# Three of eight groups of w_down as seven products in chained PSUM banks, on a hybrid decoder trunk

## The chip, the cores and the metric

The kernel runs on one core of one Trainium2 chip. The metric is the device time of one execution in microseconds (us); the lower, the better.

## The reference

Two layers of a decoder trunk over 576 token columns (512 of a prompt, 64 of eight samples). Each layer mixes the tokens with four kinds of heads and then runs an MLP of 1024 to 4096 to 1024. The change touches the MLP alone:

```python
x = x + jnp.einsum('ble,ed->bld', mix, P['w_out'][li])
h2 = rmsnorm(x, P['norm_mlp_w'][li])
up = jnp.einsum('bld,df->blf', h2, P['w_up'][li])
x = x + jnp.einsum('blf,fd->bld', jnp.square(jax.nn.relu(up)), P['w_down'][li])
```

## The kernel before

**Layout and arithmetic.** Activations lie with features on the 128 partitions and the 576 columns in the free dimension, in two halves of `TH` = 288. `x` is eight tiles of 128 features. Every fp32 operand of a large product is split into a high part (ScalarE casts it to fp32r) and a low part (VectorE subtracts the high part), and one 128x128 block of a product is three matmuls: high by high, high by low, low by high, each over 288 columns.

**The MLP.** There are 32 tiles of hidden features ("middle tiles"). `mlp` makes them two at a time (a pair, 16 pairs a layer); four of them are a group, and `w_down` is applied group by group, eight groups a layer, one group behind the pairs that are being made. The last group of the last layer goes through `last_down`, which also does the final norm.

**w_up.** The first three pairs of a layer are made plainly (`up_tile`). The other 13 go through `up_pair`: a pair is a 2 by 2 arrangement (two middle tiles, two halves of columns), and seven products of 12 matmuls replace eight (Strassen's form as Winograd orders it). The sums of weights are made on VectorE (lines 1085 to 1088), the sums of activations once a layer (`quads`). Each of the seven products has a PSUM bank of its own out of five in rotation (`bank`); VectorE adds the products into the four quarters (`add`, line 1108), multiplies by the norm's factor under a relu (line 1111), and ScalarE squares (line 1147). The halves are split and stored as `fh`, `fl`.

**w_down.** Per group there are four weight blocks (`m2`) of 128x1024. For each, `down` makes four products of 12 matmuls (two output tiles, two halves). Each has a PSUM bank out of three in rotation (`mmbank`), and VectorE adds the bank to `x` (line 1037).

**Order and buffers.** A scheduler sets each engine's order when the program is built; the order is fixed then, and every engine works through its queue in that order. `high_priority` moves the splits and the take-up of banks ahead. A raw weight tile (SyncE's queue loads it) has three buffers (`raw`), a split plain weight two (`hi`, `lo`), the split weights of `up_pair` three (`uh`, `ul`), its last one (`vh`, `vl`) and its sums (`s`) one.

Of the kernel before, what the change touches and what calls it, by code (L numbers as in the profile page):

```python
# [10 lines left out]
F32 = mybir.dt.float32  # L11
# [8 lines left out]
DEPTH = 2  # L20
# [21 lines left out]
PLAIN, QUADS = 3, 1  # L42
SA, SC = 1, 2
# [105 lines left out]
class Kern:  # L149
# [481 lines left out]
    def dt_proj(self):  # L631
# [410 lines left out]
    def quads(self, P):  # L1042
# [3 lines left out]
        for k in range(4):  # L1046
# [5 lines left out]
            t1 = P.t(("U", "W", "T1a", "T1b")[k], TH)  # L1052
# [18 lines left out]
    def up_pair(self, P, i, Q, rstd):  # L1071
# [3 lines left out]
        hl = lambda n, w, b: (P.t(n + "h", [w, 128], F32R, b), P.t(n + "l", [w, 128], F32R, b))  # L1075

        def split(hl, src):
            S.copy(hl[0], src)  # L1078
            V.tensor_tensor(hl[1], src, hl[0].bitcast(F32), op=ALU.subtract)
            return hl  # L1080

        with self.tc.high_priority(HP):
            a = split(hl("u", 8, 3), ra)
            s = P.t("s", [8, 128])
            V.tensor_tensor(s[:, :4], rb[:, :4], rb[:, 4:], op=ALU.add)
            V.tensor_tensor(s[:, 4:], s[:, :4], ra[:, :4], op=ALU.subtract)
            V.tensor_tensor(rb[:, :4], ra[:, :4], rb[:, :4], op=ALU.subtract)
            V.tensor_tensor(ra[:, 4:], ra[:, 4:], s[:, 4:], op=ALU.subtract)
            s = split(hl("u", 8, 3), s)
            b = split(hl("u", 8, 3), rb)  # L1090
            d = split(hl("v", 4, 1), ra[:, 4:])

        out = [[self.fp.t(n, dt=F32R, bufs=8) for n in ("fh", "fl")] for _ in range(2)]
        rs = [rstd[:, :TH], rstd[:, TH:]]

        def mul(n, w, o, q):
            ps = self.bank(n)
            j = 0
            for k in range(4):
                (wh, wl), (xh, xl) = (t[:, o + k] for t in w), Q[q][k]  # L1100
                for u, x in ((wh, xh), (wh, xl), (wl, xh)):
                    nc.tensor.matmul(ps[:, :TH], u, x, start=j == 0, stop=j == 11)  # L1102
                    j += 1
            return ps[:, :TH]

        def add(out, x, y):
            with self.tc.high_priority(HP):
                V.tensor_tensor(out, x, y, op=ALU.add)

        def relu(c, m, h):  # L1110
            V.scalar_tensor_tensor(c, c, 0.0, rs[h], op0=ALU.max, op1=ALU.mult)
            self.square(c, out[m], h)
# [282 lines left out]
```

## Time and profile before

| | us |
|---|---|
| median of three runs (1357.02 to 1363.0) | 1357.02 |
| the profiled execution | 1355.2 |
| its span, first to last instruction | 1353.4 |
| PE (matmul) busy | 1328.0 (98% of the span) |
| PEld (weight load) busy | 1279.6 (95%) |
| DVE (VectorE) busy | 1028.5 (76%) |
| ACT (ScalarE) busy | 658.2 (49%) |

The span is what the trace covers; 1.8 us of the profiled execution lie around it. An engine's busy time is the sum of its instructions' times, overlaps counted once. Matmuls overlap one another, so a busy PE says that it is never without one, and not how fast they follow each other; that is read from the starts in the timeline. "A <- B" in a view of waits says that A's engine stood idle until B was done.

### The profile page before, as it was taken

What the parts mean: (1) busy time and instruction counts of PE and PEld (TensorE: products, weight loads), DVE (VectorE), ACT (ScalarE), POOL (GpSimd) and SP (SyncE); (2) the same over time, 40 slices, a digit from 0 to 9 for tenths busy, and PEclk for the clock granted to TensorE, in tenths of its full rate; (3) what the DMA queues carried; (4) which work ended last, traced back from release to release, by engine and by line L of the source; (5) the groups of instructions that cost most, each with busy time, mean ns of one, the idle gap of its engine ahead of it and who ended that gap; (6) DMA issues with size and microseconds to landing.
All of it is one profiled execution on the core that took longest, in us unless ns stands there. A gap on an engine that the chain in (4) does not pass through costs nothing.

```text
span 1353.4 us, 25452 instructions
## 1 busy us (share of the span) xinstructions
PE 1328.0 (98%) x10384; PEld 1279.6 (95%) x10384; DVE 1028.5 (76%) x2043; ACT 658.2 (49%) x1175; POOL 63.3 (5%) x126
## 2 busy tenths in 40 slices
PE   7999999999999999999999999999999999999997
PEld 7999899799999999999999998988999999999997
DVE  7788888488678677776669678886977677777755
ACT  6565436766243334333354774477653243334325
POOL 2201102000000000000000001100000000000000
PEclk9999999999999999999999999999999999999999
DMA  6324414123213222322331233231223213222312
GB/s 237 104 87 139 165 68 144 48 79 110 77 65 110 78 92 81 113 75 86 131 121 47 98 117 128 94 111 48 79 81 123 78 63 109 79 82 91 115 58 71
DMA packets 39831, 131.36 MB, mean 97 GB/s; under 512 B 6089, under 2 KB 8241, under 8 KB 39681
## 3 DMA queue, kind: packets, MB, share of 16 engines
q1 hardware_dynamic: 29312, 102.12, 21.9%
q0 software_dynamic: 6512, 22.64, 5.0%
q10 hardware_dynamic: 3888, 4.97, 1.2%
q8 instruction: 82, 1.34, 0.4%
q14 instruction: 37, 0.30, 0.1%
HBM read 120.32 MB, written 11.34 MB: 97 GB/s over the span
## 4 chain that ended last, share of the span: by engine, by line
PE 86%; DVE 7%; ACT 3%; issue 2%; DMA 0%; SPq 0%; DVEq 0%; ACTq 0%
PE pd L339 33%; PE p L1102 21%; PE pi L339 15%; PE pu L339 6%; PE pl L1255 2%; PE sc L554 2%; DVE lo L326 1%; DVE a L444 1%; PE ss L402 1%; PE ao L354 1%; ACT hi L326 1%; DVE A L562 1%; DVE qE L550 1%; PE y L354 1%; PE lg L978 1%
## 5 line engine op out<-in xcount | busy, mean ns | idle before, releaser
L326 ACT CAST hi<-raw 128x1024 fp32r<-128x1024 f32 x134 | 140.2, 1046 | 297.1 <-PE pd L339 144.6
L339 PE MATMUL pd<-fh,hi 128*128 128x288 f32 x960 | 284.1, 296 | 0.0
L339 PE MATMUL pd<-fl,hi 128*128 128x288 f32 x960 | 284.0, 296 | 0.0
L339 PE MATMUL pd<-fh,lo 128*128 128x288 f32 x960 | 282.8, 295 | 0.0
L339 PE MATMUL pi<-xh,hi 128*128 128x288 f32 x704 | 210.6, 300 | 7.6 <-ACT xh L377 7.1
L339 PE MATMUL pi<-xl,hi 128*128 128x288 f32 x704 | 210.4, 300 | 1.1 <-DVE xl L378 1.1
L339 PE MATMUL pi<-xh,lo 128*128 128x288 f32 x704 | 211.1, 300 | 0.0
L326 DVE TENSOR_TENSOR lo<-raw,hi 128x1024 fp32r<-128x1024 f32 x134 | 163.6, 1222 | 27.3 <-ACT hi L326 26.7
L1037 DVE TENSOR_TENSOR x<-x,pd 128x288 f32<-128x288 f32 x240 | 108.2, 451 | 97.9 <-PE pd L339 97.8
L339 PEld LDWEIGHTS pd<-fh,lo 128*128 128x128 f32 x960 | 180.9, 188 | 0.0
L339 PEld LDWEIGHTS pd<-fh,hi 128*128 128x128 f32 x960 | 180.4, 188 | 0.0
L339 PEld LDWEIGHTS pd<-fl,hi 128*128 128x128 f32 x960 | 180.4, 188 | 0.0
L339 PEld LDWEIGHTS pi<-xh,hi 128*128 128x128 f32 x704 | 133.0, 189 | 10.1 <-ACT xh L377 7.1
L339 PEld LDWEIGHTS pi<-xh,lo 128*128 128x128 f32 x704 | 132.9, 189 | 6.0 <-issue 5.2
L339 PEld LDWEIGHTS pi<-xl,hi 128*128 128x128 f32 x704 | 132.9, 189 | 3.6 <-DVE xl L378 1.7
L1102 PE MATMUL p<-Th,ul 128*128 128x288 f32 x312 | 92.2, 296 | 0.0
L1102 PE MATMUL p<-Tl,uh 128*128 128x288 f32 x312 | 92.1, 295 | 0.0
L1102 PE MATMUL p<-Th,uh 128*128 128x288 f32 x312 | 92.0, 295 | 0.0
L1102 PE MATMUL p<-xl,uh 128*128 128x288 f32 x312 | 91.9, 295 | 0.0
L1102 PE MATMUL p<-xh,ul 128*128 128x288 f32 x312 | 91.9, 295 | 0.0
L1102 PE MATMUL p<-xh,uh 128*128 128x288 f32 x312 | 91.7, 294 | 0.0
L1078 ACT CAST uh<-raw 128x1024 fp32r<-128x1024 f32 x52 | 54.5, 1048 | 66.8 <-PE p L1102 43.2
(489 smaller groups left out, 3003.2 us busy)
## 6 DMA issues: line engine op xcount, KB each, us to landing
raw<-in_wu SPq DMA_DIRECT2D x64, 512.0 KB, 3.3
raw<-in_wd SPq DMA_DIRECT2D x64, 512.0 KB, 4.2
raw<-in_wi SPq DMA_DIRECT2D x44, 512.0 KB, 3.3
raw<-in_wo SPq DMA_DIRECT2D x16, 512.0 KB, 3.2
x<-in_xT SPq DMA_DIRECT2D x8, 288.0 KB, 5.9
a<-acd ACTq DMA_DIRECT2D x4, 576.0 KB, 4.5
xl<-in_xT POOLq DMA_DIRECT2D x8, 288.0 KB, 4.3
xd<-x POOLq DMA_DIRECT2D x8, 288.0 KB, 2.4
```

The source lines that it names most:

```text
L326: self.split_ins = nc.scalar.copy(hi, raw).ins, nc.vector.tensor_tensor(lo, raw, hi.bitcast(F32), op=ALU.subtract).ins
L339: self.nc.tensor.matmul(out, w, x[:, a], start=n == 0, stop=n == last)
L354: self.nc.tensor.matmul(out, w, x, start=n < 2, stop=n >= len(products) - 2, skip_group_check=True)
L402: nc.tensor.matmul(ps[:, :TH], ones, s[:, TH * h : TH * h + TH], start=n == 0, stop=n == len(sqs) - 1)
L444: V.scalar_tensor_tensor(dst[:, :CW], src[:, k : k + CW], w(k), dst[:, :CW], op0=ALU.mult, op1=ALU.add)
L550: V.tensor_tensor(qE[r, d, : W // 2].rearrange("p (n h) -> p n h", h=h), qu[r], eu[r], op=ALU.mult)
L554: nc.tensor.matmul(pv[:, :, 64 * ci : 64 * ci + 64], kE[:, 128 * ci : 128 * ci + 128], qE[:, :, 64 * ci : 64 * ci + 64], start=True, stop= ...
L562: V.copy_predicated(Av[:, d], m, ps[:, d].rearrange("p (n h) -> p n h", h=h))
L1037: self.nc.vector.tensor_tensor(y[:, a], x[:, a], ps, op=ALU.add)
L1078: S.copy(hl[0], src)
L1102: nc.tensor.matmul(ps[:, :TH], u, x, start=j == 0, stop=j == 11)
L1255: nc.tensor.matmul(ps, u[:, o + q], v[:, a], start=j == 0, stop=j == 11)
```

## The change

**w_down.** In groups 1, 3 and 5 (`SEVEN`) of each layer a weight block is applied by `group_seven`: the two pairs of middle tiles are the two steps of the sum over features, the output is two tiles by two halves, and seven products of six matmuls each replace the eight of that size that `down` makes in four banks. In this text the products of one block are A1, B2, A3, C4, A5, C6, A7, in the order of the code. They share three banks: A1, A3, A5 and A7 accumulate in one bank (`dA`), C4 and C6 in another (`dC`). After each product VectorE adds the bank as it stands to a quarter of `x`, and the next product of the chain goes on accumulating in the same bank. So a block has 42 matmuls and seven adds, where it had 48 and four. The sums of weights are made in place in the raw tile (`sums`, four instructions of 256 columns) and split besides (`vh`, `vl`, 768 columns, one buffer).

**The middle tiles.** A pair is now one tile of up to seven blocks (`Hh`, `Hl`, three buffers of pairs). For the three groups `finish` makes, besides the four squared quarters, three sums of them (four subtractions of 288 columns) and splits all seven. For the other groups the four quarters are split in two instructions of 576 columns. In `mlp` group g is applied after pair 2g + 2 was made (before: after pair 2g + 3).

**w_up.** `up_pair` has three banks in place of seven products' own: four products accumulate in `A`, two in `C`, one is in `B`. After each of A's first three products ScalarE copies the bank as it stands (`U1`, `U`, `W`), and A goes on accumulating. VectorE makes three adds and three relu instructions a pair (before: seven and four).

**Besides.** Two tiles move to another pool (`w4`, `dtq`), the scratch of the software DMA is halved, the output tiles of `last_down` take the buffers of `Th` and `Tl`, and `w_down`'s rows are laid out by pairs.

The diff, cut to its core:

```diff
+SEVEN = (1, 3, 5)
 ...
+    def mul(self, ps, w, o, xs, last=True, first=True):
+        j, n = 0, 3 * len(xs) - 1
+        for k, (xh, xl) in enumerate(xs):
+            wh, wl = (t[:, o + k] for t in w)
+            for u, x in ((wh, xh), (wh, xl), (wl, xh)):
+                self.nc.tensor.matmul(ps, u, x, start=first and j == 0, stop=last and j == n, skip_group_check=True)
+                j += 1
+    def sums(self, s, r, n):
+        V = self.nc.vector
+        q = lambda t, i: t[:, n * i : n * i + n]
+        V.tensor_tensor(q(s, 0), q(r[1], 0), q(r[1], 1), op=ALU.add)
+        V.tensor_tensor(q(s, 1), q(s, 0), q(r[0], 0), op=ALU.subtract)
+        V.tensor_tensor(q(r[1], 0), q(r[0], 0), q(r[1], 0), op=ALU.subtract)
+        V.tensor_tensor(q(s, 2) if n == 2 else q(r[0], 1), q(r[0], 1), q(s, 1), op=ALU.subtract)
 ...
     def up_pair(...):
-        U, W = P.t("U", TH), P.t("W", TH)
-        p1 = mul("p1", a, 0, "B11")
-        c00 = self.half_tile(P)
-        with self.tc.high_priority(HP):
-            S.copy(c00, p1)
-        add(U, c00, mul("p6", s, 4, "T2"))
-        p5 = mul("p5", s, 0, "T1")
-        add(W, U, p5)
 ...
+        self.mul(A, a, 0, Q["B11"], last=False)
+        keep(U1, A)
+        self.mul(B, a, 4, Q["B21"])
+        add(0, 0, U1, B)
+        relu(quad(0, 0), quad(0, 0), rstd[:, :TH])
+        self.mul(A, s, 4, Q["T2"], last=False, first=False)
+        keep(U, A)
+        self.mul(C, b, 0, Q["T3"], last=False)
+        self.mul(A, s, 0, Q["T1"], last=False, first=False)
+        keep(W, A)
+        add(1, 1, W, C)
+        self.mul(A, d, 0, Q["B22"], first=False)
+        relu(quad(0, 1), A, rstd[:, TH:T])
+        self.mul(C, b, 4, Q["T4"], first=False)
+        add(1, 0, U, C)
+        relu(c[1], c[1], rstd[:, :T])
 ...
+    def group_seven(self, P, g, pairs):
+        for m2 in range(KD // 2):
+            raw = self.raw(self.I["wd"][self.li, g, m2])
+            a = [... for n in ("hi", "lo")]
+            s = P.t("s", [8, 128])
+            d = P.t("vh", [6, 128], F32R), P.t("vl", [6, 128], F32R)
+            with self.tc.high_priority(HP):
+                self.sums(s, (raw[:, :4], raw[:, 4:]), 2)
+                self.split(*a, raw)
+                self.split(*d, s[:, :6])
+            A, B, C = (self.mmbank(n)[:, :TH] for n in ("dA", "dB", "dC"))
+            self.mul(A, a, 0, q(0), last=False)
+            self.add_to(x1[:, :TH], A)
+            self.mul(B, a, 2, q(1))
+            self.add_to(x1[:, :TH], B)
+            self.mul(A, d, 2, q(4), last=False, first=False)
+            self.add_to(x2[:, :TH], A)
+            self.mul(C, a, 4, q(5), last=False)
+            self.add_to(x2[:, TH:T], C)
+            self.mul(A, d, 0, q(3), last=False, first=False)
+            self.add_to(x2[:, TH:T], A)
+            self.mul(C, a, 6, q(6), first=False)
+            self.add_to(x2[:, :TH], C)
+            self.mul(A, d, 4, q(2), first=False)
+            self.add_to(x1[:, TH:T], A)
```

**What moves on the engines.** PE, w_down, layer 0. Before, in group 0, one product's last matmuls and the next one's first, in another bank (`pd` with its number):

```order
L339 MATMUL pd_583_4072<-fl_531_3697,hi581_4054 128x288
L339 MATMUL pd_583_4072<-fh_530_3696,lo581_4055 128x288
L339 MATMUL pd_584_4086<-fh_480_3414,hi581_4054 128x288
L339 MATMUL pd_584_4086<-fl_481_3415,hi581_4054 128x288
L339 MATMUL pd_584_4086<-fh_480_3414,lo581_4055 128x288
L339 MATMUL pd_584_4086<-fh_486_3472,hi581_4054 128x288
L339 MATMUL pd_584_4086<-fl_487_3473,hi581_4054 128x288
```

After, in group 1, its second block: the end of A3, what is left of C4, the start of A5 (`dA`, `dC` are the banks, `H` the middle tiles, `vh`/`vl` the split sums of weights, `hi`/`lo` the split weights):

```order
L1078 MATMUL dA_618_4490<-Hh_574_4155,vh_616_4480 128x288
L1078 MATMUL dA_618_4490<-Hl_575_4156,vh_616_4480 128x288
L1078 MATMUL dA_618_4490<-Hh_574_4155,vl_617_4481 128x288
L1078 MATMUL dC_620_4492<-Hl_575_4156,hi614_4477 128x288
L1078 MATMUL dC_620_4492<-Hh_574_4155,lo614_4478 128x288
L1078 MATMUL dA_618_4490<-Hh_526_3738,vh_616_4480 128x288
L1078 MATMUL dA_618_4490<-Hl_527_3739,vh_616_4480 128x288
L1078 MATMUL dA_618_4490<-Hh_526_3738,vl_617_4481 128x288
```

Between two uses of one bank there were two other products of 12 matmuls; here there are two matmuls, the rest of C4 having moved ahead of A3.

DVE, same group 0, before: adds of banks (`x<-x,pd`), a plain weight's low part (`lo`), sums of weights of a pair to come (`s`):

```order
L1037 TENSOR_TENSOR x_438_3113<-x_438_3113,pd_583_4072 128x288
L1037 TENSOR_TENSOR x_442_3117<-x_442_3117,pd_584_4086 128x288
L1037 TENSOR_TENSOR x_442_3117<-x_442_3117,pd_585_4100 128x288
L326 TENSOR_TENSOR lo593_4179<-raw592_4176,hi593_4178 128x1024
L1037 TENSOR_TENSOR x_439_3114<-x_439_3114,pd_588_4120 128x288
L1037 TENSOR_TENSOR x_439_3114<-x_439_3114,pd_589_4134 128x288
L1037 TENSOR_TENSOR x_443_3118<-x_443_3118,pd_590_4148 128x288
L1085 TENSOR_TENSOR s_608_4308<-raw605_4302 128x512
L1086 TENSOR_TENSOR s_608_4308<-s_608_4308,raw604_4300 128x512
```

After, group 1, from the add of A7 of the first block to the add of A5 of the second:

```order
L1194 TENSOR_TENSOR x_438_3113<-x_438_3113,dA_610_4423 128x288
L461 TENSOR_TENSOR lo614_4478<-raw613_4475,hi614_4477 128x1024
L461 TENSOR_TENSOR vl_617_4481<-s_615_4479,vh_616_4480 128x768
L1194 TENSOR_TENSOR x_439_3114<-x_439_3114,dA_618_4490 128x288
L1086 TENSOR_TENSOR s_623_4546<-raw621_4542 128x256
L1194 TENSOR_TENSOR x_439_3114<-x_439_3114,dB_619_4491 128x288
L1087 TENSOR_TENSOR s_623_4546<-s_623_4546,raw621_4542 128x256
L1194 TENSOR_TENSOR x_443_3118<-x_443_3118,dA_618_4490 128x288
L1194 TENSOR_TENSOR x_443_3118<-x_443_3118,dC_620_4492 128x288
L1088 TENSOR_TENSOR raw621_4542<-raw621_4542 128x256
L1089 TENSOR_TENSOR s_623_4546<-raw621_4542,s_623_4546 128x256
L1194 TENSOR_TENSOR x_443_3118<-x_443_3118,dA_618_4490 128x288
```

The adds, one in two instructions before, now share the queue with sums and splits of the same group: the low parts `lo` and `vl` of the next block stand between the add of A7 and that of the next A1.

ACT, layer 0, before: the one copy of a bank a pair (`COPY` from `p1`), then weight casts:

```order
L1118 COPY T_622_4344<-p1_621_4331 128x288
L1078 CAST uh_634_4454<-raw632_4450 128x1024
L326 CAST hi667_4664<-raw666_4662 128x1024
L1078 CAST uh_637_4463<-s_636_4458 128x1024
L1078 CAST vh_641_4471<-raw632_4450 128x512
L1078 CAST uh_639_4467<-raw633_4452 128x1024
L1118 COPY u650_4494<-p1_649_4481 128x288
```

After, the three copies from the bank `pA` of the first pair that follows a plain group, and weight casts of the next pair (`uh`):

```order
L1146 COPY U1_580_4162<-pA_577_4159 128x288
L460 CAST uh_587_4278<-raw585_4274 128x1024
L1146 COPY U_581_4163<-pA_577_4159 128x288
L460 CAST uh_590_4287<-s_589_4282 128x1024
L1146 COPY W_582_4164<-pA_577_4159 128x288
L460 CAST vh_594_4295<-raw585_4274 128x512
```

Two copies more a pair; the third one (`W`) stands behind the cast of `uh`.

## Rows read from the trace of the kernel before

**Rows 1.** The page: span, busy time and share of each engine, the chain by engine.

```profile
span 1353.4 us, 25452 instructions
PE 1328.0 (98%) x10384; PEld 1279.6 (95%) x10384; DVE 1028.5 (76%) x2043; ACT 658.2 (49%) x1175; POOL 63.3 (5%) x126
...
PE 86%; DVE 7%; ACT 3%; issue 2%; DMA 0%; SPq 0%; DVEq 0%; ACTq 0%
```

**Rows 2.** Waits of PE, longest first: waiting line <- releaser: total us, times, longest.

```profile
PE pi L339 <- ACT xh L377: 7.1, 1, 7.1
...
PE pd L339 <- ACT mixh L1008: 0.9, 2, 0.5
```

**Rows 3.** Timeline of PE, end of a down group, start of a pair: start us, us.

```profile
463.25 0.29 PE L339 MATMUL pd<-fh,lo 128*128 128x288 f32 x1
463.38 0.29 PE L1102 MATMUL p<-xh,uh 128*128 128x288 f32 x1
...
464.82 0.30 PE L1102 MATMUL p<-xh,ul 128*128 128x288 f32 x1
...
472.00 0.29 PE L1102 MATMUL p<-xh,vl 128*128 128x288 f32 x1
```

**Rows 4.** Timelines of DVE and ACT there: the work that takes up PE's results.

```profile
463.58 0.46 DVE L1037 TENSOR_TENSOR x<-x,pd 128x288 f32<-128x288 f32 x1 [0.44 <-PE pd L339]
...
465.16 0.40 ACT L1118 COPY T1a<-p 128x288 f32<-128x288 f32 x1 [1.36 <-PE p L1102]
...
468.22 1.05 ACT L1078 CAST uh<-raw 128x1024 fp32r<-128x1024 f32 x1 [2.67 <-PE p L1102]
469.17 1.04 ACT L326 CAST hi<-raw 128x1024 fp32r<-128x1024 f32 x1
```

**Rows 5.** Timeline of DVE, back to back instructions of several widths.

```profile
568.43 0.45 DVE L1108 TENSOR_TENSOR U<-U,p 128x288 f32<-128x288 f32 x1
568.79 0.45 DVE L1108 TENSOR_TENSOR u<-W,p 128x288 f32<-128x288 f32 x1
569.21 0.69 DVE L1079 TENSOR_TENSOR vl<-raw,vh 128x512 fp32r<-128x512 f32 x1
569.82 1.22 DVE L326 TENSOR_TENSOR lo<-raw,hi 128x1024 fp32r<-128x1024 f32 x1
570.96 0.45 DVE L1108 TENSOR_TENSOR T<-U,p 128x288 f32<-128x288 f32 x1
```

**Rows 6.** The same, of 256 columns, and of 576 (a group: count, busy us, mean ns).

```profile
49.45 0.41 DVE L542 TENSOR_TENSOR t<-c 128x256 f32<-128x256 f32 x1
49.78 0.42 DVE L545 TENSOR_TENSOR c<-c 128x256 f32<-128x256 f32 x1
...
L392 DVE TENSOR_TENSOR ssq<-ssq,sq 128x576 f32<-128x576 f32 x28 | 21.1, 752 | 0.1
```

**Rows 7.** Timelines of PE, ACT and DVE where PE resumes after a wait.

```profile
17.88 0.40 PE L339 MATMUL pi<-xh,hi 128*128 128x288 f32 x1 [0.53 <-ACT hi L326]
18.12 0.30 PE L339 MATMUL pi<-xl,hi 128*128 128x288 f32 x1
...
16.80 1.03 ACT L326 CAST hi<-raw 128x1024 fp32r<-128x1024 f32 x1
...
9.04 0.61 PE L339 MATMUL pi<-xl,hi 128*128 128x288 f32 x1 [1.13 <-DVE xl L378]
...
8.18 0.81 DVE L378 SCALAR_TENSOR_TENSOR xl<-x,prm,xh 128x576 fp32r<-128x576 f32 x1
```

**Rows 8.** A plain down group: stretch; PE, PEld, DVE, ACT, POOL busy; clock, DMA share, GB/s.

```profile
440.00:463.00 23.00, 23.00 (x176) 23.00 (x175) 16.43 (x29) 5.48 (x8) 0.00 (x0) 1.00 0.28 92
```

**Rows 9.** DMA issues: median us from issue to landing.

```profile
raw<-in_wu SPq DMA_DIRECT2D x64, 512.0 KB, 3.3
raw<-in_wd SPq DMA_DIRECT2D x64, 512.0 KB, 4.2
...
x<-in_xT SPq DMA_DIRECT2D x8, 288.0 KB, 5.9
```

More of the change, by code (lines that the diff above doesn't have):

```diff
@@ L1073, in up_pair, with halves, split @@
+    def halves(self):
+        self.uid += 1
+        return [self.np_.tile([128, T], F32, name=f"c{m}_{self.uid}", tag="sq", bufs=SQB) for m in range(2)]
+    def up_pair(self, P, i, Q, rstd, seven):
         nc, V, S, li = self.nc, self.nc.vector, self.nc.scalar, self.li
         ra, rb = (self.raw(self.I["wu"][li, f]) for f in (2 * i, 2 * i + 1))
[L1075 to L1079, printed above, removed]
+        def split(src):
+            hl = (P.t("uh", [8, 128], F32R, 3), P.t("ul", [8, 128], F32R, 3))
+            self.split(*hl, src)
@@ L1090, in up_pair @@
[L1090 to L1104, printed above, removed]
@@ new lines, in relu @@
+        def relu(out, x, r):
+            with self.tc.high_priority(HP):
+                V.scalar_tensor_tensor(out, x, 0.0, r, op0=ALU.max, op1=ALU.mult)
+        A, B, C = (self.bank(n)[:, :TH] for n in ("pA", "pB", "pC"))
+        U1, U, W = P.t("U1", TH), P.t("U", TH), P.t("W", TH)
+        self.mul(A, a, 0, Q["B11"], last=False)
[4 more added lines that the diff above has]
+        self.mul(A, s, 4, Q["T2"], last=False, first=False)
@@ new lines, in up_pair, with up_plain, put @@
+        keep(U, A)
[8 more added lines that the diff above has]
+        relu(c[1], c[1], rstd[:, :T])
+        self.finish(P, H, c, seven)
+        return H
+    def up_plain(self, P, i, seven):
+        V = self.nc.vector
+        H, c = self.pair_tiles(), self.halves()
+        for m in range(2):
+            wh, wl = self.weight(self.I["wu"][self.li, 2 * i + m])
+            def put(half, a, ps, m=m):
+                with self.tc.high_priority(HP):
+                    V.scalar_tensor_tensor(c[m][:, a], ps, 0.0, self.rs[:, a], op0=ALU.max, op1=ALU.mult)
+            self.product("pu", [(wh[:, k], wl[:, k], self.xh[k], self.xl[k]) for k in ORDER], put)
+        self.finish(P, H, c, seven)
+        return H
@@ new lines, in add_to, with columns, group_plain @@
+    def add_to(self, x, ps):
+        with self.tc.high_priority(HP):
+            self.nc.vector.tensor_tensor(x, x, ps, op=ALU.add)
+    def columns(self, pairs, h):
+        return [tuple(t[:, (0, 3, 1, 2)[2 * m + h]] for t in H) for m in range(2) for H in pairs]
+    def group_plain(self, g, pairs):
+        for m2 in range(KD // 2):
+            w = self.weight(self.I["wd"][self.li, g, m2])
+            for m in range(2):
+                for h in range(2):
+                    ps = self.mmbank("pd")[:, :TH]
+                    self.mul(ps, w, 4 * m, self.columns(pairs, h))
+                    self.add_to(self.x[m2 + 4 * m][:, TH * h : TH * h + TH], ps)
@@ L1251, in last_down @@
                 ps = self.mmbank("pl")[:, :w]
-                j = 0
-                for q, (h, l) in enumerate(xs):
-                    for u, v in ((wh, h), (wh, l), (wl, h)):
-                        nc.tensor.matmul(ps, u[:, o + q], v[:, a], start=j == 0, stop=j == 11)
-                        j += 1
+                self.mul(ps, (wh, wl), o, self.columns(pairs, c // TH))
                 x = self.x[k][:, a]
```

138 lines of the change are left out of this document (65 added, 73 removed).

## The prediction

> **What bounds the kernel now.** I read the page first: PE is busy for 1328.0 of 1353.4 us, and the chain that ended last runs on PE for 86% [rows 1]. Busy PE alone says little, so the timeline came next: 67 matmuls in a row start between 463.25 and 472.00, across the border from w_down to w_up, so 8.75 / 66 = 0.1326 us from start to start [rows 3]. The view of PE's waits shows in which stages that rate breaks: the longest wait is 7.1 us at the first projection, and for `pd` there is one row, 0.9 us behind the attention's output, in the out projection [rows 2]. So in the MLP PE issues matmuls without a break, and what counts there is how many there are and whether each finds its operands and its bank. DVE and ACT have room on average: in a plain down group DVE is busy for 16.43 of 23 us, ACT for 5.48 [rows 8].
>
> **What the change removes.** A plain group is 16 products of 12 matmuls, 192; a changed one is 4 blocks of 42, 168. Six groups (three in each layer) save 6 x 24 = 144 matmuls, 144 x 0.1326 = 19.1 us [rows 3], all on the path. The Trainium skill ("TensorE: Matmul & The Clock Gate", Back-to-back issue gap) gives N / 2.4 + 2.5 ns for the isolated gap at full clock, 122.5 ns for 288 columns. By it the saving would be 17.6 us; the trace's 132.6 ns decides.
>
> **What a hand-over costs.** In a chain PE must not go on in a bank before DVE or ACT has read it. From the start of a product's last matmul to the start of its add it is 0.33 us (463.25 and 463.58), to that of ACT's copy 0.34 (464.82 and 465.16); the add takes 0.46, the copy 0.40 [rows 3, 4]. PE's next instruction starts 0.05 after the releaser's end (DVE 8.18 + 0.81, PE 9.04; ACT 16.80 + 1.03, PE 17.88), and the matmul behind a wait is followed by the next after 0.24 us and not 0.13, so a wait costs 0.11 more than its length [rows 7]. Together 0.33 + 0.46 + 0.05 + 0.11 = 0.95 us for an add, 0.90 for a copy. With n other matmuls in between, PE would come back after (n + 1) x 0.1326: six just cover an add (0.93), two (0.40) leave a wait of 0.55.
>
> **The down blocks.** DVE's cost in a full queue is from start to start: 0.36 for 288 columns, 0.61 for 512, 1.14 for 1024 [rows 5], 0.33 for 256, and 0.75 - 0.08 = 0.67 for 576 [rows 6]. 768 columns do not occur; between 512 (0.69 long) and 1024 (1.22) [rows 5] I take the middle, 0.96 long and 0.87 in a queue. Now one block, the second to the third of a group, in the order that the program has. Zero is A3's first matmul.
> A3's last starts at 0.66, its add ends at 0.66 + 0.33 + 0.46 = 1.45, A5 begins at 1.61 where it would have begun at 1.06: only two matmuls are between. Wait 0.55.
> A5, C6: the add of A5 is over as A7 begins, 3.20; A7's last starts at 3.86, its add lasts to 4.65.
> Behind that add stands `lo` of the next block: its sums stood among this block's adds, so `hi` is done and DVE is the limit. It runs from 4.57 to 5.79, and PE may use it from 5.95. Till then PE has ten matmuls that need `hi` alone, and C4's first two have to wait 0.14 for A7's bank; it is through at about 5.47. Wait about 0.5.
> `vl` follows to 6.67 (its `vh` has one buffer and could not be written before A7's last matmul), then the add of A1. A1's last matmul starts at 6.35, so that add ends at 7.14, and A3 of the next block begins at 7.3, as its predecessors end.
> The period is 7.3 us for 46 matmuls (four of the next pair among them), 6.1 us without waits: 1.2 lost.
> From the first to the second block DVE has two more instructions of 576 columns in place of one (0.67 more), and the sums, so `hi`, come later: 1.6 by the same steps. From the third to the fourth 53 matmuls cover more, 0.6. In the fourth, nine or ten matmuls stand between the uses of the bank: none. Into the first, the splits of `vh` and `vl` follow the pair's last use of that buffer: 0.3. A group loses 3.7 us, six lose 22.2.
> The lower bound is what DVE must do if it never idles: from add of A1 to add of A1, 7.19 us in block one, 6.52 in block two, 6.99 in block three (the same durations, in the order's counts), against 6.10, 6.10 and 7.03 us of matmuls: 1.09 + 0.42 = 1.5 a group, 9 in all. The upper bound takes half as much again as the walk, 33.
> The Trainium skill ("Perfetto Trace Analysis", Matmuls) wants independent matmul groups to rotate through PSUM banks, so that taking up one overlaps the next group's matmuls. The plain groups do, and no `pd` row waits for DVE [rows 2]; by that rule the waits above stay, and only their size is open.
>
> **The pairs.** Seven adds and four relus become three and three; with the splits in wider instructions DVE is freed of about 11 - 6 = 5 instructions of 0.36 a pair, which PE does not feel (it never waited there) [rows 2]. New on PE's path are ACT's copies. The first two have a product of 12 matmuls behind them, 13 x 0.1326 = 1.72 against 0.90: covered unless a cast of 1024 columns (1.05) [rows 4] just began. After T1 the order leaves four matmuls in 19 of 26 pairs: 0.90 - 0.66 = 0.24 each, 4.6 us. In seven there are nine or ten, but in ACT's queue a cast of `uh` stands before the copy of `W`, and its buffer is freed by the same product: 0.34 + 0.95 (casts follow at that distance [rows 4]) + 0.40 + 0.16 = 1.85 against 1.46, 0.39 each, 2.7. Together 7.3; from 0 (ACT ahead everywhere) to twice that, 15.
>
> **At no cost.** `finish` for three groups (four subtractions, three more splits) lies beside the next pair's 84 matmuls (11.1 us), a pair less than before; without that cover the wait would be at A1 of the group. The two tiles in another pool, the halved scratch (POOL's queue alone; no row of PE's waits names POOL or a DMA [rows 2]) and the last tiles' buffers: 0, at most 2 us if POOL's loads for the out projection came late.
>
> **The sum.** -19.1 + 22.2 + 7.3 = +10.4 on the profiled execution's 1355.2: 1365.6. The median stands 1.8 above that execution, so 1367.4; I say 1367.
>
> **Rivals.**
> *DVE keeps up* (faster). The waits shrink to what DVE must do, since one instruction's wait fills the next one's: 9 us, the pairs' copies hidden. -19.1 + 9 = -10: 1347. For it: DVE's share is 76% [rows 1]. Against: a chain of add, product, add makes DVE idle while PE works, and the bound has no idling. It decides if the period of block two is 6.5 and not 7.3.
> *Only the down blocks wait* (no change). ACT, at 49% [rows 1], has its copies done in time: -19.1 + 22.2 = +3: 1360. Against: the cast before the copy is in the order and the four matmuls do not cover even an idle ACT.
> *Raw tiles come late* (slower). A raw tile is now held through sums, cast and `lo`, and the pair's next raw tile is asked for only when `lo` of the first block ends, 5.8; ACT casts it before `hi` of the block after next. With a landing of 3.3 to 4.2 us [rows 9] it is just in time; with 5.9, as loads of `x` show [rows 9], two blocks a group wait 1.5 more: 18 us, 1385.
> *It does not do what it says*: the built order has 144 matmuls fewer, which leaves next to nothing for this.
>
> **How the numbers follow.** A measurement tells 0.5% (6.8 us) from no change: 1350.2 and 1363.8 are the borders. Forecast 1367: 0.50; only the blocks, 1360: 0.24; DVE keeps up, 1347: 0.15; raw tiles, 1385: 0.10; the rest 0.01. So slower 0.60, same 0.25, faster 0.15. The range leaves out a part of the second-last two: 1349 to 1381, about one in ten on each side.
>
> **What the profile after would show.** Right: PE's waits have new rows, `dA` and `dC` behind DVE, with single waits of 0.3 to 1 us, some 20 to 25 us in all in six places, and `pA` behind ACT's copies, 5 to 10; the number of matmuls is 144 lower; busy PE falls below 98%; the clock stays at full rate, since no wait is long. DVE is busy for 9 of 10 parts in the six groups. Wrong: `dA` rows under 10 us in all (then DVE keeps up), no `pA` rows (then 1360), or waits of ACT for raw tiles that end PE's (then 1385). The whole is wrong at its root if PE's starts no longer follow at 0.1326 us.

## The result, and the profile after

The changed kernel takes **1372.29 us** (median of 4 runs, 1371.32 to 1373.78), the kernel before 1357.02: a ratio of 1.0107, 95% interval 1.008 to 1.0134, so it is slower by 15.3 us. The forecast was 1367 us, slower, in a range of 1349 to 1381; all of the result lies inside it. The profiled execution took 1372.96 us, its span is 1371.2.

The page of the changed kernel (span; busy time, share and count of each engine; chain that ended last, by engine), to be read against [rows 1]:

```profile
span 1371.2 us, 25216 instructions
PE 1332.5 (97%) x10240; PEld 1265.0 (92%) x10240; DVE 1087.0 (79%) x2113; ACT 692.6 (51%) x1147; POOL 63.5 (5%) x126
...
PEclk9999999999999999999999999999999999999999
...
PE 84%; DVE 9%; ACT 4%; issue 2%; DMA 1%; DVEq 0%; ACTq 0%
```

PE has 10240 matmuls and had 10384: the 144 are gone, and the granted clock is full in every slice. Yet the span is 17.8 us longer, and the chain has moved from PE to DVE (7 to 9%) and ACT (3 to 4%). The view of PE's waits names the new ones (line waiting <- releaser: total us, times, longest); before, none of them was there [rows 2]:

```profile
PE dA L1078 <- DVE lo L461: 4.9, 12, 0.6
...
PE dA L1078 <- DVE x L1194: 3.4, 12, 0.3
...
PE dA L1078 <- ACT hi L460: 2.1, 6, 0.4
```

This view counts only time in which no matmul is running. A matmul's row is 0.29 us long and the next starts after 0.1326 [rows 3], so the first 0.16 us of each wait stand in no row, nor does the slow restart. What counts is how late each matmul starts. I therefore add up, over PE's timeline, by how much the distance from one start to the next exceeds 0.1326 us (only where the excess is over 0.02), and call this **late starts**. Between neighbouring matmuls of 288 columns they grow over the whole kernel from 26.4 us to 62.4, by 36.0; with -19.1 for the 144 matmuls this makes +16.9 of the span's +17.8.

By stretch: from the first `pu` matmul of a layer to the last matmul of its MLP, layer 0 went from 387.66 to 395.73 us and layer 1 from 388.78 to 396.21, +15.5 together, close to the change of the medians. The six changed groups have 24.4 us of late starts (4.0 to 4.1 each, all alike), the rest of the two MLPs 12.1 (before 1.5). A group is counted from its first matmul to its last, with those of a pair that stand among them: 22.6 of the 24.4 us stand at `dA` and `dC`, 1.8 at `pA`.

One block in detail. PE's timeline of the changed kernel, first group, from the end of the first block's A7 into the second block, then A3 of blocks two and three (start us, us; in brackets idle time and releaser):

```profile
386.98 0.30 PE L1078 MATMUL dA<-Hh,vl 128*128 128x288 f32 x1
387.63 0.40 PE L1078 MATMUL dA<-Hh,hi 128*128 128x288 f32 x1 [0.35 <-ACT hi L460]
387.87 0.29 PE L1078 MATMUL dA<-Hl,hi 128*128 128x288 f32 x1
...
388.53 0.29 PE L1078 MATMUL dC<-Hl,hi 128*128 128x288 f32 x1
389.42 0.40 PE L1078 MATMUL dA<-Hh,lo 128*128 128x288 f32 x1 [0.60 <-DVE lo L461]
...
390.85 0.37 PE L1078 MATMUL dA<-Hh,vh 128*128 128x288 f32 x1
...
391.58 0.30 PE L1078 MATMUL dA<-Hh,vl 128*128 128x288 f32 x1
391.72 0.29 PE L1078 MATMUL dC<-Hl,hi 128*128 128x288 f32 x1
391.85 0.29 PE L1078 MATMUL dC<-Hh,lo 128*128 128x288 f32 x1
392.43 0.40 PE L1078 MATMUL dA<-Hh,vh 128*128 128x288 f32 x1 [0.28 <-DVE x L1194]
...
398.21 0.37 PE L1078 MATMUL dA<-Hh,vh 128*128 128x288 f32 x1
```

The first `hi` matmul comes 0.65 us after its predecessor, so 0.52 late, and its own follower 0.24 later, another 0.11: 0.63. `lo` is 0.76 + 0.11 late, A5 at 392.43 is 0.45 + 0.11 late, with two matmuls of C4 between it and A3. From A3 to A3 the period of the second block is 398.21 - 390.85 = 7.36 us.

DVE's timeline beside it (same kernel), with the row of ACT that gives `hi`:

```profile
386.08 0.42 DVE L1088 TENSOR_TENSOR raw<-raw 128x256 f32<-128x256 f32 x1
386.42 0.42 DVE L1089 TENSOR_TENSOR s<-raw,s 128x256 f32<-128x256 f32 x1
386.75 0.45 DVE L1194 TENSOR_TENSOR x<-x,dC 128x288 f32<-128x288 f32 x1
387.12 0.75 DVE L461 TENSOR_TENSOR Hl<-c,Hh 128x576 fp32r<-128x576 f32 x1
387.78 0.45 DVE L1194 TENSOR_TENSOR x<-x,dA 128x288 f32<-128x288 f32 x1
388.15 1.22 DVE L461 TENSOR_TENSOR lo<-raw,hi 128x1024 fp32r<-128x1024 f32 x1
389.28 0.95 DVE L461 TENSOR_TENSOR vl<-s,vh 128x768 fp32r<-128x768 f32 x1
...
391.92 0.46 DVE L1194 TENSOR_TENSOR x<-x,dA 128x288 f32<-128x288 f32 x1 [0.18 <-PE dA L1078]
...
386.53 1.05 ACT L460 CAST hi<-raw 128x1024 fp32r<-128x1024 f32 x1 [1.56 <-DVE raw L1088]
```

No row from 386.08 to 389.28 has an idle time: DVE is the queue in which `lo` stands, and `hi` waits for the third sum (ends at 386.50; ACT starts at 386.53). At 391.92 it is the other way round: DVE waits for A3, then PE waits for DVE. That is a hand-over. Two kinds of waits alternate, then, and the experiments ask which of them is the price. The windows view tells how full DVE is in this group (stretch; PE, PEld, DVE, ACT, POOL busy):

```profile
377.91:410.77 32.86, 31.14 (x219) 29.22 (x218) 30.91 (x61) 13.85 (x18) 0.00 (x0) 1.00 0.17 58
```

30.91 of 32.86 us, 94%; in a plain group it was 16.43 of 23, 71% [rows 8].

### The profile page after: what moved, and what is told of

It reads as the page before. It is cut to its first block, busy times and chain, and to the rows that moved or that the text cites. A ratio compares the mean times of both kernels' runs of the same rounds, so it can differ in the third digit from the quotient of the medians.

```text
span 1371.2 us, 25216 instructions
## 1 busy us (share of the span) xinstructions
PE 1332.5 (97%) x10240; PEld 1265.0 (92%) x10240; DVE 1087.0 (79%) x2113; ACT 692.6 (51%) x1147; POOL 63.5 (5%) x126
## 4 chain that ended last, share of the span: by engine, by line
PE 84%; DVE 9%; ACT 4%; issue 2%; DMA 1%; DVEq 0%; ACTq 0%
PE pi L340 17%; PE pd L1078 16%; PE pA L1078 12%; PE pC L1078 6%; PE pu L340 6%; PE dA L1078 5%; PE pd L340 4%; PE pB L1078 3%; PE sc L555 2%; PE dC L1078 2%; PE pl L1078 2%; DVE x L1194 2%; PE dB L1078 1%; DVE lo L461 1%; PE ss L403 1%
## 5 line engine op out<-in xcount | busy, mean ns | idle before, releaser
L1078 PE MATMUL pd<-Hl,hi 128*128 128x288 f32 x576 | 169.7, 295 | 0.1
L1078 PE MATMUL pd<-Hh,lo 128*128 128x288 f32 x576 | 169.2, 294 | 0.0
L1078 PE MATMUL pd<-Hh,hi 128*128 128x288 f32 x576 | 168.6, 295 | 0.0
L1078 PEld LDWEIGHTS pd<-Hl,hi 128*128 128x128 f32 x576 | 108.2, 188 | 0.5 <-DVE Hl L461 0.4
L1078 PEld LDWEIGHTS pd<-Hh,lo 128*128 128x128 f32 x576 | 108.4, 188 | 0.0
L1078 PEld LDWEIGHTS pd<-Hh,hi 128*128 128x128 f32 x576 | 107.7, 188 | 0.5 <-DVE x L1194 0.2
L340 PE MATMUL pd<-mixl,hi 128*128 128x288 f32 x256 | 77.2, 302 | 0.0
L340 PE MATMUL pd<-mixh,hi 128*128 128x288 f32 x256 | 76.2, 302 | 0.9 <-ACT mixh L1009 0.9
L340 PE MATMUL pd<-mixh,lo 128*128 128x288 f32 x256 | 76.8, 301 | 0.0
L461 DVE TENSOR_TENSOR ul<-raw,uh 128x1024 fp32r<-128x1024 f32 x54 | 65.8, 1219 | 3.6 <-ACT uh L460 3.6
```

What stands on the lines that cost most here:

```text
L340: self.nc.tensor.matmul(out, w, x[:, a], start=n == 0, stop=n == last)
L461: self.nc.vector.tensor_tensor(l, src, h.bitcast(F32), op=ALU.subtract)
L1078: self.nc.tensor.matmul(ps, u, x, start=first and j == 0, stop=last and j == n, skip_group_check=True)
```

## The experiments

Each kernel was timed in turn with the kernel before on the same chip. "MLP" is the change of the two MLP stretches against the kernel before, in one profiled execution; it follows the medians within about 1 us. The changed kernel's own interval is wide, and those of e5, e7 and e8 overlap it, as that of e12 overlaps that of e10: their gains of two to four us are not clear of noise by the medians alone, and the MLP column, one execution each, is the second witness.

| kernel | median us | minus before | ratio, 95% interval | MLP | late, six groups | late, rest of MLPs |
|---|---|---|---|---|---|---|
| before | 1357.02 | | | | | 1.5 |
| changed | 1372.29 | +15.3 | 1.0107 (1.008 to 1.0134) | +15.5 | 24.4 | 12.1 |
| e1 pairs alone | 1365.00 | +7.7 | 1.0062 (1.0046 to 1.0078) | +8.8 | | 11.2 |
| e2 groups alone | 1370.68 | +13.4 | 1.0105 (1.0086 to 1.0124) | +13.5 | 32.0 | 3.1 |
| e3 neither | 1357.59 | +0.3 | 1.0003 (0.9993 to 1.0013) | +0.3 | | 3.1 |
| e4 moved tiles in before | 1357.66 | +0.3 | 1.0006 (0.9995 to 1.0017) | +0.1 | | 1.6 |
| e5 `lo` earlier | 1368.94 | +12.1 | 1.0089 (1.0074 to 1.0104) | +12.6 | 19.6 | 14.1 |
| e6 sums on GpSimd | 1395.06 | +38.2 | 1.0282 (1.0265 to 1.0299) | +39.0 | 33.5 | 26.8 |
| e7 own bank in a pair | 1370.00 | +13.1 | 1.0099 (1.0084 to 1.0114) | +13.8 | 24.7 | 10.5 |
| e8 own banks in a block | 1368.01 | +11.2 | 1.0081 (1.0066 to 1.0096) | +11.8 | 13.7 | 19.7 |
| e9 no sums | 1360.59 | +3.8 | 1.0034 (1.0022 to 1.0046) | +3.8 | 14.2 | 10.7 |
| e10 e5 and e7 | 1365.95 | +9.1 | 1.0065 (1.005 to 1.008) | +9.1 | 19.9 | 10.5 |
| e11 e8 and e9 | 1358.27 | +1.6 | 1.0011 (1.0 to 1.0023) | +1.0 | 11.0 | 11.3 |
| e12 e10, a sum on GpSimd | 1363.94 | +7.3 | 1.0055 (1.004 to 1.007) | +6.9 | 17.9 | 10.6 |

### One part at a time: e1 to e4

e1 leaves w_down's groups plain, e2 gives each of w_up's products a bank of its own again, e3 does both:

```diff
-SEVEN = (1, 3, 5)
+SEVEN = ()
```

```diff
-        A, B, C = (self.bank(n)[:, :TH] for n in ("pA", "pB", "pC"))
...
+        keep(c00, prod("p1", a, 0, "B11"))
+        plus(U, c00, prod("p6", s, 4, "T2"))
+        plus(W, U, prod("p5", s, 0, "T1"))
...
```

> The changed kernel with no group of w_down in seven products (SEVEN empty), w_up chained as in the change. My theory: the parts add up. In the trace of the changed kernel the matmul starts of the six groups are late by 24.4 us in all, against 19.1 us of matmuls saved, so without them 5.3 us go: 1367, 10 above the kernel before, left by the copies of the chained pairs (about 8) and the middle tiles that come late for plain groups (about 3). Rival: the pairs' waits are there only because DVE and ACT are loaded by the groups; then 1357 to 1360.

> The changed kernel with w_up's seven products in banks of their own again, the three groups in seven products kept. My theory: the copies' waits (about 8 us) go, the groups keep their 24.4: 1364. Rival: the chained w_up is what frees DVE for the groups (five instructions of 0.36 us a pair, 1.8 us); without it the groups' waits grow by that much at each of the two pairs round a group, 20 us in all, and the time is 1372 or more.

> The changed kernel with neither: w_up's products in own banks, all groups of w_down plain. What is left of the change is the pairs' tiles, one pair less between a pair and its group, and the moved tiles. My theory: PE's late starts at pd and pl (about 3 us) and up to 2 us ahead of the MLP stay: 1360 to 1362. Rival: nothing is left, 1357.

e4 puts into the kernel before only the two tiles' new pool and the smaller scratch:

```diff
-        w4 = self.small([128, KD, 32], "w4", 1)
+        w4 = self.hp.t("w4", [KD, 32])
...
-        self.dtq = self.small([128, T], "dtq", 1)
+        self.dtq = self.hp.t("dtq")
...
-... dynamic_dma_scratch_size=8192)
+... dynamic_dma_scratch_size=4096)
```

> The kernel before with only the two tiles in the other pool and the scratch of the software DMA halved. The MLP of the first layer began 1.9 us later in the changed kernel's trace. My theory: this is their cost: 1359, and the first w_up matmul at about 294 us in place of 292. Rival: it is the spread between two executions, 1357.

Chaining w_up costs 1365.00 - 1357.59 = **7.4 us**, give or take about 2.5 by the two intervals; the term of the prediction was 7.3. e1 lies between its theory (1367) and its rival (1357 to 1360). e3 and e4 cannot be told from the kernel before: the moved tiles, the scratch and the new order of middle tiles cost nothing that the medians show, as forecast, and my expectation of 1360 to 1362 for e3 was wrong. Of the changed kernel's profile I had taken the part from the first matmul to the first MLP (286.82 us against 284.92) for a cost of the tiles. e4's median says that it is none. Its profile cannot tell: it has 290.85 there, but in that execution (1361.36 us) the granted clock was 0.94 and 0.89 of full speed in the windows from 140 to 160 and from 160 to 180 us.

e2 is what the prediction had not foreseen; it comes near its rival's 1372. Groups alone cost +13.1 us over e3, with the pairs 7.4 should have been added, but both together cost 14.7. The waits of PE in e2:

```profile
PE dA L1078 <- DVE x L1200: 8.8, 22, 0.5
PE dA L1078 <- DVE lo L461: 5.9, 12, 0.6
```

With own banks a pair has seven adds and four relus on DVE again in place of three and three, and a group is late by 5.3 us, not 4.05. So the chained w_up gives about 1.3 us a group back: the two halves of the change are not independent. The growth stands at A5, the hand-over: in the four blocks of e2's first group it is 0.68, 0.69, 0.42 and 0.80 us late, in the changed kernel 0.03, 0.56, 0.55 and nothing. The fourth block's in e2 (PE's row):

```profile
407.55 0.40 PE L1078 MATMUL dA<-Hh,vh 128*128 128x288 f32 x1 [0.54 <-DVE x L1200]
```

Two things changed there at once. DVE has more to do for a pair, and the built order has only 12 matmuls of a pair among a group's 168 where the changed kernel has 50, so that less stands between the uses of a bank. How much of the 1.3 us is DVE's relief and how much is this cover, no run separates.

### Order and hand-overs: e5, e7, e10

e5 lets the next block's sums, `hi` and `lo` be asked for ahead of a block's last two adds, and holds the add of A7 until `lo` is issued:

```diff
+            if m2 < KD // 2 - 1:
+                nxt = self.group_weights(P, g, m2 + 1)
+                self.lo_next = nxt[2]
+            self.add_to(x2[:, :TH], C)
+            self.add_to(x1[:, TH:T], A, late=True)
```

> The changed kernel with VectorE's queue in another order at one place: the low part of the next block's weights stands ahead of the add of A7, not behind it. Nothing else is computed. My theory: the order of the queue (a split between the last add of a block and the first of the next) makes the wait of A1's second half, 0.77 and 0.37 us and 0.11 for each restart, and delays the next A3; moved, a group's waits fall from 4.05 us to about 2.5: 9 us less, 1363. Rival: DVE's work in a block (6.5 to 7.2 us against 6.1 us of matmuls) sets the period whatever the order; then 1370 to 1373. A third way: A7's add comes later by the 1.1 us of the split and holds C4's bank; then slower than 1373.

It gains 3.4 us, between theory and rival: groups are 3.2 us late. Where the second block begins nothing changes. PE's rows of e5 there:

```profile
386.76 0.40 PE L1078 MATMUL dA<-Hh,hi 128*128 128x288 f32 x1 [0.35 <-ACT hi L1217]
...
388.19 0.40 PE L1078 MATMUL dA<-Hh,lo 128*128 128x288 f32 x1 [0.62 <-DVE lo L1218]
```

The group begins at 377.05 us here and at 377.91 in the changed kernel. Counted from there, `hi` is used at the same time (9.71 and 9.72 us) and `lo` only 0.37 earlier, while four matmuls that need `hi` alone stand ahead of it in place of six: PE waits as long. The later blocks lose their wait for `lo`.

e7 gives the product behind T1 a bank of its own, so that PE need not wait for the copy `W`; one add more for a pair:

```diff
-        self.mul(A, d, 0, Q["B22"], first=False)
-        relu(quad(0, 1), A, rstd[:, TH:T])
+        D = self.bank("pD")[:, :TH]
+        self.mul(D, d, 0, Q["B22"])
+        add(0, 1, W, D)
+        relu(quad(0, 1), quad(0, 1), rstd[:, TH:T])
```

> The changed kernel with one link of w_up's chain cut: the product after T1 gets a bank of its own, and VectorE makes one add more a pair (26 x 0.36 = 9 us of DVE's time). My theory: PE's wait for the copy of W (19 x 0.24 + 7 x 0.39 = 7.3 us by the forecast) goes nearly whole, the groups keep their 24: 1365 to 1367. Rival: the added DVE work lengthens the groups' waits as own banks did (5.3 against 4.05 us a group): 1369 or more.

It gains only 2.3 us: the rival's number, and a little of its mechanism, since the late starts at the groups' own matmuls grow from 22.6 to 24.2 us. Those at `pA` fall from 7.7 us to 1.5, but 3.1 appear at the new bank `pD`, six times behind ACT's `vh`: behind the copy that PE no longer waits for, the next operand is hardly earlier.

```profile
PE pD L1078 <- ACT vh L460: 2.1, 6, 0.4
```

e10 has both edits.

> The changed kernel with both of the edits that gained: the next block's `lo` goes ahead of the last add of a block on VectorE, and a pair's product of the sixth place has a bank of its own (one add more for a pair). If the two are independent: 1372.3 - 3.4 - 2.3 = 1366.6, groups 3.2 us each and 5.0 to 5.5 us of other late starts in each layer. Rival (both lean on the same VectorE: the 26 adds more push `lo` back again, or the earlier `lo` pushes the pairs' adds back): 1368 to 1370, groups above 3.5 or the rest above 6.

1365.95, where 1366.6 was expected: the two add up, as far as the intervals can tell.

### DVE's work against hand-overs: e6, e8, e9, e11

e6 moves the four sums of a block to GpSimd:

```diff
-        V = self.nc.vector
+        V = self.nc.gpsimd if n == 2 else self.nc.vector
```

> The changed kernel with the four sums of weights of a block (256 columns each) on GpSimd in place of VectorE. DVE is freed of 4 x 0.33 = 1.3 us a block, and the cast and split no longer wait for sums that stand among the adds. If DVE's capacity is what the blocks wait for, a group's waits fall by up to 1.1 + 0.4 us for the first two blocks and the time by about 9: 1363. If the hand-overs (product, add, next product in the same bank) are what they wait for, the time stays within 3 us of 1372. If GpSimd is slow at this, over 1.5 us each, weights come late: over 1376.

This ended at 1395.06, the third case by its time, though no sum took 1.5 us. Two of the groups of GpSimd's instructions by line in e6 (count, busy us, mean ns, idle before), and PE's waits:

```profile
L1088 POOL TENSOR_TENSOR raw<-raw 128x256 f32<-128x256 f32 x24 | 26.2, 1092 | 0.0
...
L1089 POOL TENSOR_TENSOR s<-raw,s 128x256 f32<-128x256 f32 x24 | 17.8, 740 | 0.0
```

```profile
PE dA L1078 <- ACT hi L460: 11.3, 12, 1.6
PE pA L1078 <- ACT U L1146: 8.4, 6, 1.4
```

A sum that takes DVE 0.42 us takes GpSimd 0.74 to 1.09, and the first three stand in a row ahead of `hi`: 0.75 + 0.84 + 1.09 = 2.7 us and not 3 x 0.42 = 1.3. `hi` is late, and with it all that stands behind it in ACT's queue, the copy `U` of the next pair too. The Trainium skill ("GPSIMD Engine Reference", Engine selection) calls GpSimd about twice as slow for two-input elementwise work and names VectorE for it; the trace agrees in the main (740 to 1092 ns against 420, 1.8 to 2.6 times). So e6 tells nothing about DVE's capacity, since it lengthened the chain that it was to relieve.

e8 and e9 are each meant to take away one of the two causes. e8: every product begins in the next of three banks.

```diff
-            self.mul(A, d, 2, q(4), last=False, first=False)
-            self.add_to(x2[:, :TH], A)
...
+                ps = self.mmbank(n)[:, :TH]
+                self.mul(ps, w, o, xs)
+                self.add_to(x, ps)
```

> The changed kernel, but each of a block's seven products begins a sum of its own in the next of three banks; the matmuls, the seven adds, the sums and the casts are the same in number and kind. It leaves out the accumulation from product to product. So what it takes away is the hand-over alone: TensorE no longer has to stay out of a bank until VectorE has read it. Theory (the waits at the fifth product and at the second are hand-overs, 0.45 + 0.11 us each, two or three in a group; the waits for `hi` and `lo` are VectorE's queue): the late starts at the fifth product go, those at hi and lo stay: groups 4.05 -> 2.6 to 2.9 us, 6 x 1.3 = 8 us less, 1363 to 1366. Rival A (VectorE's work in the block sets the period, the waits are only where it shows): what goes at the fifth product comes back at lo, groups 3.7 to 4.2, 1370 to 1374. Rival B (lo is late only because the adds ahead of it are held up by hand-overs): nearly all of the group's waits go, under 1.2 us a group, 1352 to 1357.

e9: no sums of weights in a block.

```diff
-                self.sums(s, (raw[:, :4], raw[:, 4:]), 2)
...
-                self.split(*d, s[:, :6])
+                self.split(*d, raw[:, :6])
```

> The changed kernel without the four sums of weights in each block: the difference weights are split from the raw tile's first six parts, so that VectorE has about 4 x 0.33 = 1.3 us less to do in each block, and `hi` no longer follows sums. Matmuls, banks, hand-overs and adds are the same. It leaves out the sums. Theory (VectorE's work and its queue order make the waits for `hi` and `lo`, about 0.63 + 0.87 + 0.47 us a group; the hand-overs at the fifth product, 0.56 twice, are not touched): groups 4.05 -> 1.3 to 2.2 us, 6 x 2.3 = 14 us less, 1356 to 1361. Rival A (hand-overs make most of it): groups stay above 3.3, 1368 to 1372. Rival B (VectorE's capacity makes all of it): groups under 0.8, and less than 1354, since pairs gain as well.

In e8 the groups get shorter by 10.8 us, 2.0 us late in five of the six (3.9 in the other): the waits at A5 are gone and do not come back at `lo`, so within the group the theory, not rival A, is right. But the kernel gains only 4.3 us. PE's waits of e8; its timelines of PE, DVE and ACT behind the first group:

```profile
PE pA L1078 <- ACT uh L460: 3.8, 7, 1.3
...
PE pC L1078 <- ACT uh L460: 3.1, 6, 0.5
```

```profile
409.30 0.40 PE L1078 MATMUL pC<-Th,uh 128*128 128x288 f32 x1 [0.52 <-ACT uh L460]
...
410.25 0.40 PE L1078 MATMUL pA<-xh,uh 128*128 128x288 f32 x1 [0.42 <-ACT uh L460]
...
407.49 0.68 DVE L1088 TENSOR_TENSOR raw<-raw,raw 128x512 f32<-128x512 f32 x1
...
408.20 1.99 ACT L460 CAST uh<-raw 128x1024 fp32r<-128x1024 f32 x2 [0.54 <-DVE raw L1088]
```

and the windows view of that group:

```profile
377.81:407.57 29.76, 28.86 (x212) 27.96 (x211) 28.75 (x58) 11.67 (x16) 0.00 (x0) 1.00 0.19 65
```

ACT stands idle until DVE's sum at 407.49 ends, and then casts `uh`; PE is through the group sooner and waits for it there, 1.48 us behind each group. DVE is busy for 28.75 of 29.76 us of the group, 97%. So what goes at the hand-overs comes back one pair later, at the same queue: rival A's mechanism, in another place than it named. The Trainium skill ("Perfetto Trace Analysis", Matmuls) says that independent groups of matmuls should rotate through PSUM banks so that reading one out overlaps the next; here e8 is that rule, and it is worth 4.3 us and not the 10.8 that leave the groups.

e9 gains 11.7 us with all hand-overs in place, twice and more what e8 gains. Its groups are 2.4 us late, and the rows left are waits for adds (PE's waits of e9):

```profile
PE dC L1078 <- DVE x L1194: 3.1, 6, 0.5
PE dA L1078 <- DVE x L1194: 1.6, 6, 0.3
```

The theory's 1356 to 1361 holds. These adds are hand-overs that DVE's queue holds up: at the second block of the first group the one of `dA` at 388.18 us starts as `lo` ends, the next at 389.42 as `vl` ends. The period of the second block is 6.49 us in e9 and was 7.36. That this is the 6.5 at which the prediction lets DVE keep up is chance: that figure was DVE's work with the sums, which e9 leaves out, and DVE idles for 0.48 and 1.15 us in that block. The 6.49 are 46 matmuls (6.10) and 0.38 us of short late starts. One thing e9 cannot tell: without the sums DVE has less to do, and `hi` need not wait for them either. No run separates the two, since e6 made the second worse.

e11 does both.

> Both at once: a bank of its own for each of a block's seven products, and no sums of weights (the accumulation and the sums are left out; 168 matmuls and 28 adds a group stay). Own banks alone moved 10.8 us of late starts out of the groups, of which 7.6 came back in the pairs behind them, where TensorE waits for the cast `uh` of w_up's weights; the sums alone gave 11.7 us. Theory (hand-overs and VectorE's work are together all that a group loses, and `uh` is late because VectorE's sums hold up the weights): groups 0.3 to 1.0 us, other late starts 5 to 6.5 us in a layer, so -19.1 + 4 + 10 on 1356.8: 1350 to 1353, the first of these kernels that is faster than before. Rival (`uh` is late because the pair's raw tile or ScalarE is late, whatever VectorE does): other late starts 9 to 10 us a layer, 1355 to 1358. If groups stay above 1.5 us, there is a third cost in them.

1358.27 is neither the theory's 1350 to 1353 nor, by its mechanism, the rival's. `uh` is no longer late (the rest of the MLPs is 5.6 us late a layer, as in e9): that part of the theory holds. But groups stay at 1.8 us each, over the 1.5 that I had set as the sign of a third cost. PE's waits and DVE's timeline of e11 name the larger part, 0.95 us a group (another 0.7 stands at the pair's matmuls among the group's):

```profile
PE dA L1078 <- DVE vl L461: 4.1, 6, 0.7
```

```profile
383.37 0.75 DVE L461 TENSOR_TENSOR Hl<-c,Hh 128x576 fp32r<-128x576 f32 x1
...
384.40 0.75 DVE L461 TENSOR_TENSOR Hl<-c,Hh 128x576 fp32r<-128x576 f32 x1
...
386.54 1.22 DVE L461 TENSOR_TENSOR lo<-raw,hi 128x1024 fp32r<-128x1024 f32 x1
387.67 0.95 DVE L461 TENSOR_TENSOR vl<-raw,vh 128x768 fp32r<-128x768 f32 x1
```

At the second block DVE has the two low parts of a pair's middle tiles, 0.75 us each, and `lo` and `vl`, 2.17, all within 5.3 us. It is a burst, not the mean: in this group DVE is busy for 86% of the time. What remains in e11 closes the account: -19.1 for the matmuls, +11.0 in groups, +9.8 in the rest (11.3 against 1.5) is +1.7, and the median is +1.6. The 19.1 us saved are real; they are spent. Own banks alone take 10.8 us out of the groups, the sums alone 10.2, both together 13.4: these are not two prices that add, but one chain through DVE's queue, shortened at two places.

### One step more: e12

```diff
-        V.tensor_tensor(q(r[1], 0), q(r[0], 0), q(r[1], 0), op=ALU.subtract)
+        (self.nc.gpsimd if n == 2 else V).tensor_tensor(q(r[1], 0), q(r[0], 0), q(r[1], 0), op=ALU.subtract)
```

> The kernel with `lo` ahead of a block's last add and a pair's own bank (1365.95), and now one of the four sums of a block, the third, on GpSimd, with VectorE doing the fourth beside it. Theory (VectorE's work is what costs: leaving out 24 x 1.3 = 32 us of it gave 11.7 us, 0.37 for one): 24 x 0.33 = 7.9 us less on VectorE gives 2.9 us, 1363. Rival (the third sum stands ahead of the cast to `hi`, and took 1.09 us on GpSimd when all four were there, against 0.33): `hi` comes 0.4 to 0.8 us later in blocks that already wait for it, 1366 to 1369.

1363.94, 2.0 us less than e10 (2.2 less in the MLPs): near the theory's 2.9, with what the rival named in it, but the intervals of the two overlap. PE's waits of e12:

```profile
PE dA L1078 <- ACT hi L1219: 4.2, 6, 0.7
...
PE dA L1078 <- DVE lo L1220: 1.4, 6, 0.2
```

`lo` waits 1.4 us where it was 3.6 in e10, and `hi` of the fourth block now waits 4.2. It is the fastest of the kernels that do all of the change, and still 0.55% slower than the kernel before. None of the runs points to one that beats it.

## Why the prediction came out as it did

**The saving: right.** 144 records fewer, at an unchanged 0.1326 us; e11's account closes with 19.1.

**The hand-over: right in kind and size.** A3's last matmul starts at 391.58, its add at 391.92 (0.34 later), lasts 0.46, PE comes 0.05 after it, the next matmul 0.11 late: 0.96, forecast 0.95. With two matmuls between, A5 waits 0.45 and loses 0.11 more, forecast 0.55. I had counted the 0.11 inside it.

**The group: right.** 3.7 us forecast, 4.05 measured, of which 3.8 at the group's own matmuls (22.2 and 22.6 in all) and 0.3 at those of a pair, which the sum has under the pairs. The second block's period was to be 7.3 and is 7.36; the first's 7.8 for 7.7, the third's 7.7 for 7.6. The wait for `lo` was put at about 0.5 from the second block to the third and is 0.47 there; from the first to the second, where the walk gives only 1.6 for all waits, it is 0.87. That most would be lost there was the walk's result. The lower bound of 1.5 a group, DVE without idling, was not reached; e11, in which DVE has 1.3 us a block less to do than the bound counts, still has 1.8.

**The pairs: right in kind, the number in part by luck.** 7.3 forecast, 7.4 measured alone (e1 against e3). By late starts the waits at the copies `W` are 6.4 us in the changed kernel: 19 of 0.22 on average, as forecast (0.24), and seven of 0.30 to 0.37, forecast 0.39. In e1 6.6 us stand at `pA`, and at `pd` and `pl` 1.6 more than in e3, which the term did not contain. The single wait was put at 0.24 with four matmuls between; PE's rows at a copy `W` of the changed kernel, with ACT's:

```profile
428.28 0.29 PE L1078 MATMUL pd<-Hl,hi 128*128 128x288 f32 x1
428.54 0.40 PE L1078 MATMUL pA<-xh,vh 128*128 128x288 f32 x1
428.77 0.29 PE L1078 MATMUL pA<-xl,vh 128*128 128x288 f32 x1
...
428.08 0.40 ACT L1146 COPY W<-pA 128x288 f32<-128x288 f32 x1 [1.96 <-PE pA L1078]
```

0.13 + 0.11 = 0.24. No `pA` row stands in the view of PE's waits, because a wait of 0.13 hides under a matmul of 0.29: the sign that I named for "then 1360" was read off a view that cannot show it. The page has it in the groups of the weight loads (PEld; count, busy us, mean ns, idle before and its releaser), 5.6 us behind `W`, where 5 to 10 were forecast:

```profile
L1078 PEld LDWEIGHTS pA<-xh,vh 128*128 128x128 f32 x104 | 19.6, 188 | 5.6 <-ACT W L1146 5.6
```

The sign for the groups (20 to 25 us of `dA` rows) has the same fault: the rows hold 10.4, the late starts 22.6. Under 10 was to mean that DVE keeps up, so the rows came within 0.4 us of a false answer.

**What was mis-sized.** Forecast +10.4 on the profiled execution, measured +17.8 there, +15.5 in the MLPs and +15.3 between medians. Of the 5 us, the groups' own matmuls are 0.4 (22.6 for 22.2) and the copies `W` -0.9 (6.4 for 7.3). The sum had nothing for two other places. At `pA` and `pC` away from the copies 2.9 us of late starts stand in the changed kernel, the longest 0.66 behind one of DVE's adds. At `pd` and `pl` it is 3.1 more than before, and all of this lies in the last group of each layer. In layer 1 (PE's row):

```profile
1334.78 0.66 PE L1078 MATMUL pl<-Hh,hi 128*128 128x288 f32 x3 [0.37 <-ACT Hh L460]
```

I had put `finish` at nothing, covered by the next pair's 84 matmuls; behind the last pair of a layer there is no next pair. For the other groups the cover holds. In e2 and e3 half of these late starts are there (1.5 more than before), in the kernels with chained pairs 2.6 to 3.1; e3's median is still the same as before within 0.1%, so their price in time is not measured apart.

**What was not foreseen.** The sum treats groups and pairs as independent; e2 shows that they are not. With own banks in the pairs a group is 5.3 us late. That the error stayed small is because the walk was made in the order that the whole change has, with the pairs' fewer instructions in DVE's queue and their matmuls among the group's.

**The rivals.** DVE keeps up (1347): fell with the period of 7.36. Only the blocks wait (1360): fell with e1. Raw tiles late (1385): a raw tile of w_down lands after 3.5 us in the changed kernel and after 4.2 before [rows 9], and no wait of PE is ended by one.

## What to carry over

Before a cheaper algorithm for a matmul-bound stretch is built, count what it adds to the engine that feeds and empties the matmuls, and lay it out in its queue block by block: here 24 matmuls fewer a group were worth 3.2 us and the adds, sums and splits cost 4. Shares over the whole kernel (76% for DVE) say nothing of it; the stretch does (94%). And when a wait is removed, look at the next consumer of the same queue before the gain is booked: in e5 4.8 us left the groups and 3.4 were gained, in e7 6.2 left `pA` for 2.3, in e8 10.8 for 4.3.

## What the runs showed of the hardware

- A matmul of 288 columns that resumes after a wait is followed by the next 0.11 us late, whether the wait was long or short: 0.76 + 0.11, 0.45 + 0.11, and 0.13 + 0.11 at the copies `W`. The changed kernel has some 40 such restarts in the MLP of a layer, 8.9 us in both; this cost shows in no row of waits.
- A sum of 256 columns took GpSimd 740 to 1092 ns on average (e6), against 0.42 us on DVE; the one that writes its own input was the slowest there, and no slower than the others on DVE. All four there cost 22.8 us (e6 against the changed kernel). One of four came out 2.0 us faster (e12 against e10), which is not clear of noise.
